# Raw x in the K, V and Q projections, the 1/rms row spread by TensorE, and one work unit per attention pair through all groups

## Chip, cores and metric

The kernel runs on all 8 cores of one Trainium2 chip (two dies, cores 0 to 3 and 4 to 7). The metric is the device time in microseconds (us) of the slowest core; "span" is a core's time from its first to its last instruction in the profiled run. A ratio is the mean time of one kernel's fast runs over the mean of the other's fast runs of the same rounds on the same chip, so it is not quite the ratio of the medians that are quoted.

## The reference, cut to what matters

Batch 4, 4096 tokens, width 1024. Two cores share a batch element: each takes every second tile of 128 queries (2048 tokens, four groups of 512), and both compute K and V for all 4096 tokens (eight blocks of 512).

```python
xn = rmsnorm(x, norm_mix_g)
u  = xn @ w_in                                # conv B,C,V | q | k | v | two gates
y_a = short_gated_conv(b_g, c_g, v_a, conv_w) @ w_a_out
o   = diff_attention(q, k, v, lam, slopes)    # 4 heads, 2 softmax maps of 64, ALiBi, causal
o   = rmsnorm(o, subln_g) * (1 - lam_init)
y_b = o @ w_b_out
x = x + (g_a * y_a + g_b * y_b) @ w_o         # g_a, g_b: sigmoid gates
h = rmsnorm(x, norm_mlp_g) @ w_mlp_in
x = x + jnp.square(jax.nn.relu(h)) @ w_mlp_out
return rmsnorm(x, norm_final_g)
```

## The kernel before

One list W holds the work other than attention as (weight, function) entries: K, V, Q and conv projections, then gates and merge. An attention group is a generator that gives control back twice per pair (one 128-key tile of both key halves against 512 queries of one head), and the loop then runs entries of W. All of them share PSUM bank 7 while a group runs; banks 0 to 3 hold scores, 4 to 6 the P·V sums. Cast loads (fp32 to bf16) go out on GpSimd's queue (`cload`), plain transfers on SyncE's (`ld`, S.dma("sp")).

```python
def row_bcast(blk, src, dst, n, p):             # the 1/rms row of a block, over HBM
    row = rr_sp[blk, 0:n]
    ...                                         # (cut)
            return e.dma_start(out=row.rearrange("(t p) -> p t", p=128), in_=src.ap[:, 0:4])
    S.dma("sp", w, [src], [key])
    ld(dst.ap, rr_sp[blk:blk + 1, 0:n].partition_broadcast(128), [dst], [key])

def prelude(blk):
    ...                                         # a: load x^T and tokens; sq: squares; r: 1/rms; b: row_bcast
    def nrm(c):                                 # x^T := x^T * gain * row, before any K, V or Q matmul
        ...
    steps = [a, sq(0), sq(1), sq(2), sq(3), r, b, nrm(0), nrm(2), nrm(4), nrm(6)]

def epilogue(h):                                # reads PSUM banks 4, 5, 6 throughout
    ...                                         # reciprocals of the row sums
    dve(... e_u = b5 * (-lam/l2) ...)
    for t in range(4):
        dve(... e_o[t] = oview(0, t) / l1 + e_u[t] ...)
    ...                                         # squares, 1/rms of the head output on GpSimd
    deferred.append((2, d1))                    # e_b = e_o * 1/rms
    deferred.append((4, d2))                    # four PE transposes, copy, store to on_sp

def merged(g, upto, ratio):
    oring[0] = Ring([7])
    credit = 0.0
    for slot in attn(g):
        run_deferred()
        credit += ratio / 2.0
        while credit >= 1.0:
            credit -= 1.0
            if done[0] < upto:
                one_chunk()
    oring[0] = ALL
PLAN = {0: ("a0", "a1", 1.4), 1: ("a1", "a2", 1.25), 2: ("a2", "a3", 0.8), 3: ("a3", "g2", 1.6)}
# after attention: all of W1 (8 MB as it lands) and W2[0] are loaded in one heap, then the rest of the gates,
# then W2[1..3], then x2 of block 0 (m_load(0)), then the MLP
```

The softmax here doesn't subtract the row's maximum and nothing guards it: scores larger than these inputs give would overflow.

## Time and profile before

| kernel before | us |
|---|---|
| median of the first runs (lowest, highest) | 1758.13 (1747.26, 1761.42) |
| first softmax exponential at | 147 |
| attention groups 0, 1, 2, 3 | 208, 197, 197, 341 |
| gates and merge left over | 207 |
| MLP | 451 |

The stage times are the stretches that the prediction shows. The page of the profile adds three lines that the prediction does not show: busy time and share of each engine, what the chain that ended last consisted of, and TensorE's granted clock in 40 equal slices of the span (tenths of full speed).

```profile
PE 1243.2 (71%) x7168; PEld 585.5 (33%) x7168; DVE 500.4 (29%) x1135; ACT 529.8 (30%) x744; POOL 61.6 (4%) x97
PE 58%; DMA 22%; DVE 10%; issue 4%; ACT 3%; POOL 1%; DVEq 0%; SPq 0%; ACTq 0%; POOLq 0%
PEclk9576567677777889776798998979769999999999
```

PE is the only engine over a third busy, and 22% of the chain is transfers. The clock reaches 9 for good only in the last quarter, the MLP.

### The profile page before, as it was taken

Reading aid. Unit: us, or ns where it says so; the run is one execution under the profiler, and the core shown is the slowest. Engines: PE = TensorE matmul, PEld = TensorE weight load, DVE = VectorE, ACT = ScalarE, POOL = GpSimd, SP = SyncE. Lnnn points to the kernel's source line nnn. Section 1 sums busy time; section 2 is a strip of 40 time slices with the busy share of each in tenths; the row PEclk is TensorE's granted clock in tenths of the full one; section 3 lists DMA queues with packets and bytes.
Section 4 is the critical chain, followed back from the end, with each engine's and each line's share of the span. In section 5 each row is a group of like instructions: output and inputs, shape, how many; then the busy total and the mean of one; then the engine's idle time right before and its main releaser. Section 6 shows DMA issues by size and latency. Waiting matters only on the chain.

```text
span 1748.7 us, 20490 instructions; the slowest of 8 cores (1730.7 to 1748.7 us)
## 1 busy us (share of the span) xinstructions
PE 1243.2 (71%) x7168; PEld 585.5 (33%) x7168; DVE 500.4 (29%) x1135; ACT 529.8 (30%) x744; POOL 61.6 (4%) x97
## 2 busy tenths in 40 slices
PE   3053255575746768785896986939439999999998
PEld 1021122232323334432343443414114444444443
DVE  1022245133433423321324234423302121221212
ACT  1011221153325635553464553212103022130220
POOL 2000000000000000000000001000000000000000
PEclk9576567677777889776798998979769999999999
DMA  8877210810312110724003014980760020120101
GB/s 169 84 83 76 69 40 19 97 56 11 85 26 55 37 11 28 111 47 102 27 35 114 1 52 133 183 209 33 161 164 13 37 85 1 48 73 37 61 1 61
DMA packets 38021, 119.57 MB, mean 68 GB/s; under 512 B 7680, under 2 KB 12160, under 8 KB 34464
## 3 DMA queue, kind: packets, MB, share of 16 engines
q0 software_dynamic: 7200, 39.91, 17.5%
q1 hardware_dynamic: 30720, 78.33, 14.0%
q8 instruction: 60, 0.98, 0.2%
q14 instruction: 41, 0.34, 0.1%
HBM read 128.77 MB, written 29.37 MB: 90 GB/s over the span
## 4 chain that ended last, share of the span: by engine, by line
PE 58%; DMA 22%; DVE 10%; issue 4%; ACT 3%; POOL 1%; DVEq 0%; SPq 0%; ACTq 0%; POOLq 0%
PE ps_all L386 57%; DMA rr_sp<-big 6%; DMA big<-rr_sp 5%; DMA big<-xs 5%; ACT big L670 2%; DMA big<-x_sp 2%; DMA x_sp<-big 1%; DMA xm_sp<-big 1%; DVE big L706 1%; DVE big L489 1%; DMA big<-xn_sp 1%; DVE big L830 1%; DVE big L710 1%; DMA big<-ya_sp 1%; DVE big L814 1%
## 5 line engine op out<-in xcount | busy, mean ns | idle before, releaser
L386 PE MATMUL ps_all<-big 128*128 128x512 bf16 (+4 forms) x6976 | 1229.5, 344 | 424.5 <-DVE big L564 66.4
L386 PEld LDWEIGHTS ps_all<-big 128*128 128x128 bf16 (+1 forms) x6976 | 573.8, 102 | 1074.5 <-issue 674.5
L670 ACT ACTIVATE big<-ps_all,big 128x1024 bf16<-128x1024 f32 (+3 forms) x384 | 320.2, 880 | 356.9 <-PE ps_all L386 340.0
L898 ACT ACTIVATE big<-ps_all 128x512 bf16<-128x512 f32 x128 | 76.4, 597 | 193.0 <-PE ps_all L386 193.0
L899 DVE TENSOR_TENSOR big<-big 128x512 bf16<-128x512 bf16 x128 | 54.4, 425 | 193.5 <-ACT big L898 193.1
L791 DVE SCALAR_TENSOR_TENSOR big<-big,ps_all 128x512 f32<-128x512 f32 x64 | 44.0, 688 | 190.0 <-PE ps_all L386 189.9
L780 ACT ACTIVATE big<-ps_all,big 128x512 f32<-128x512 f32 x64 | 44.0, 687 | 154.7 <-PE ps_all L386 154.7
L489 DVE SCALAR_TENSOR_TENSOR big<-big 128x512 bf16<-128x512 bf16 x56 | 39.2, 745 | 171.4 <-DMA big<-rr_sp 171.4
L915 ACT ACTIVATE big<-big 128x1024 bf16<-128x1024 f32 x16 | 16.9, 1057 | 208.3 <-DVE big L910 208.3
L430 ACT ACTIVATE big<-big 128x1024 bf16<-128x1024 f32 x32 | 33.8, 1057 | 129.1 <-DMA big<-xs 129.1
L910 DVE SCALAR_TENSOR_TENSOR big<-ps_all,big 128x512 f32<-128x512 f32 x32 | 24.0, 751 | 163.2 <-PE ps_all L386 163.2
L715 POOL TENSOR_TENSOR big<-big 128x4 f32<-128x4 f32 x16 | 16.2, 1015 | 784.5 <-DVE big L713 600.7
L818 ACT ACTIVATE big<-big 128x1024 bf16<-128x1024 f32 x16 | 16.9, 1057 | 81.2 <-DVE big L814 81.2
L675 DVE TENSOR_TENSOR big<-big 128x256 bf16<-128x256 bf16 x64 | 18.6, 290 | 73.6 <-ACT big L670 73.5
L814 DVE SCALAR_TENSOR_TENSOR big<-ps_all,big 128x512 f32<-128x512 f32 x32 | 22.1, 689 | 59.1 <-PE ps_all L386 35.0
L605 DVE TENSOR_TENSOR big<-ps_all,big 128x512 f32<-128x512 f32 x16 | 11.1, 692 | 87.5 <-PE ps_all L386 74.0
L828 PE MATMUL ps_all<-big 128*128 128x128 bf16 x128 | 10.5, 229 | 35.0 <-DVE big L817 30.4
L537 DVE CAST big<-ps_all 128x512 bf16<-128x512 f32 x32 | 21.8, 690 | 46.4 <-PE ps_all L386 46.4
L727 PE MATMUL ps_all<-big 128*128 128x128 bf16 x64 | 7.1, 242 | 38.0 <-DVE big L720 36.7
L554 DVE CAST big<-ps_all 128x512 bf16<-128x512 f32 x28 | 19.4, 691 | 29.7 <-PE ps_all L386 29.5
L830 DVE TENSOR_TENSOR big<-ps_all,big 128x1024 bf16<-128x1024 bf16 x16 | 19.6, 1224 | 23.4 <-DMA x_sp<-big 18.0
L917 POOL TENSOR_TENSOR big<-big 128x1 f32<-128x1 f32 x16 | 8.7, 543 | 459.5 <-DVE big L916 459.5
(69 smaller groups left out, 328.7 us busy)
## 6 DMA issues: line engine op xcount, KB each, us to landing
big<-xs SPq DMA_DIRECT2D x48, 512.0 KB, 4.5
xm_sp<-big SPq DMA_DIRECT2D x16, 512.0 KB, 2.9
big<-w POOLq DMA_DIRECT2D x8, 1024.0 KB, 34.3
big<-w POOLq DMA_DIRECT2D x4, 2048.0 KB, 24.2
big<-xm_sp SPq DMA_DIRECT2D x16, 512.0 KB, 4.7
out<-big SPq DMA_DIRECT2D x16, 512.0 KB, 2.6
big<-xT POOLq DMA_DIRECT2D x14, 512.0 KB, 15.6
xn_sp<-big SPq DMA_DIRECT2D x4, 1024.0 KB, 4.1
```

Source lines behind the costliest of these rows:

```text
L386: S.op("pe", lambda e: e.matmul(out, lhsT, rhs, start=start, stop=stop, skip_group_check=skip), reads, writes)
L430: act(lambda e: e.activation(junk.ap, xt.ap, AF.Square, accum_out=ss1[blk].ap[:, t:t + 1]), [xt], [junk, ss1[blk]])
L489: dve(lambda e, k=k: e.scalar_tensor_tensor(x[k].ap, x[k].ap, ccol(C_GMIX + k), R_b.ap, ALU.mult, ALU.mult), [x[k], cst, R_b], [x[k]])
L537: dve(lambda e: e.tensor_copy(dst.ap, ps), [key], [dst])
L670: act(lambda e, a=a, b=b, c=c, s=s, PT=PT, scale=scale: e.activation(PT.ap[:, :, a:b], Sb[s][:, :, a:b], AF.Exp, bias=ccol(C_BTAB + c), sc ...
L780: act(lambda e: e.activation(t.ap, ps, AF.Tanh, bias=hbg.ap[:, 8 * w + dm:8 * w + dm + 1], scale=0.5), [key, hbg], [t])
L791: dve(lambda e: e.scalar_tensor_tensor(t.ap, t.ap, 1.0, ps, ALU.add, ALU.mult), [key, t], [t])
L814: dve(lambda e: e.scalar_tensor_tensor(x.ap[:, hs], ps, 0.5, x.ap[:, hs], ALU.mult, ALU.add), [key, x], [x])
L830: dve(lambda e: e.tensor_tensor(g_x2.ap, pb, ccol(C_GMLP, 8).unsqueeze(2).to_broadcast([128, 8, 128]), ALU.mult), [key, cst], [g_x2])
L898: act(lambda e: e.activation(r.ap, ps, AF.Relu), [key], [r])
L899: dve(lambda e: e.tensor_tensor(h2[fc].ap, r.ap, r.ap, ALU.mult), [r], [h2[fc]])
L910: dve(lambda e: e.scalar_tensor_tensor(x.ap[:, hs], ps, r2q[b].ap[:, t:t + 1], x.ap[:, hs], ALU.mult, ALU.add), [key, x, r2q[b]], [x])
```

## The change

Its intent is to take the waits out of everything before the MLP. (1) K, V and Q use raw x; the gain is folded into the weights, and 1/rms is applied as results leave PSUM (V; Q; K of blocks 1 to 3) or as the exponential's scale (K of blocks 0, 4 to 7). (2) The row of 1/rms is spread over partitions by four small matmuls. Squares run one block ahead. (3) One unit of other work per pair, from the first pair to the last. (4) The epilogue copies the sums out of PSUM at once and does its arithmetic later. (5) SBUF is laid out per head, so W1 can come in as heads of group 3 end; all first loads are queued at once.

```diff
-N_DMA_SEMS = 12
+N_DMA_SEMS = 24
 ...
+    def bcast(blk):
+        def f():
+            ps, key = obank()
+            for t in range(4):
+                mm(ps[:, t * 128:(t + 1) * 128], rs1[blk].ap[:, t:t + 1].to_broadcast([128, 128]),
+                   ccol(C_ID, 128), t == 0, t == 3, [rs1[blk], cst], [key], skip=True)
+            dve(lambda e: e.tensor_copy(R_b.ap, ps), [key], [R_b])
 ...
+    def fold_gain(w, c):
+        dve(lambda e: e.tensor_scalar_mul(w[c].ap, w[c].ap, ccol(C_GMIX + c)), [w[c], cst], [w[c]])
+    def k_evac(blk, h, ps, key):
+        dst = KT[blk][h]
+        if blk in ksc:
+            dve(lambda e: e.tensor_copy(dst.ap, ps), [key], [dst])
+        else:
+            dve(lambda e: e.tensor_tensor(dst.ap, ps, R_b.ap, ALU.mult), [key, R_b], [dst])
 ... (V times rs1 and Q times R_b as they leave PSUM; block 4's K straight behind the loads)
+        for m in range(2):                                    # epilogue: three copies, L686 and L688
+            dve(lambda e, m=m: e.tensor_copy(o[:, m, 0:3, 0:129], bank(4 + m)... ), [pk(4 + m)], [o_raw])
+        dve(lambda e: e.tensor_copy(o[:, :, 3, 0:129], bank(6)... ), [pk(6)], [o_raw])
 ... (d0: combine the two maps; d1: squares and 1/rms; d2: product, L714; d3: transposes L722, copy, store)
+        deferred.extend([(1, d0), (2, d1), (4, d2), (5, d3)])
 ...
+    W += spread(qs(0), stats(5, 1))
+    mark(0)
+    W += spread(ks(5) + vs(5), [wc_load(0), wc_load(1)] + normed(0) + [lambda: xT_load(2, 2)])
+    W += spread([], stats(1, None))
+    W += [(0.2, bcast(1))]
+    W += spread(ks(1) + vs(1) + qs(1), [halo_load, wc_load(2), wc_load(3), halo_stat] + ...)
+    mark(1)
+    W += [(0.2, halo_norm)] + [(0.4, halo_chunk(ch)) for ch in range(4)]
+    W += spread(conv(0), normed(1) + stats(2, 6))
+    W += [(0, lambda: xT_load(6, 1)), (0.2, bcast(2))]
 ... (blocks 2, 6, 3, 7 in the same way)
+    W += [(0, g_w1)] + [(1, f) for f in conv(3)]
+    W += [(0, lambda: g_loads(0))]
+    W += [(1, f) for f in conv(2)] + [(0, g_w2)]
+    mark("G")
+    W += [(0, lambda: g_loads2(0))]                           # reload of attention and conv outputs, on_sp, ya_sp
+    W += G_list(0, 1) + G_list(1, 2) + G_list(2, 3)
+    mark("G3")
+    W += G_list(3, None)
 ...
+    for n, p in enumerate(pairs):
+        if n + 1 < len(pairs):
+            if pairs[n + 1]["g"] != p["g"]:
+                until(pairs[n + 1]["g"])                      # flush what the next group needs
+            qk(n + 1)
+            ex(n + 1)
+        pv(n, 0)
+        other(limit, 0.5)
+        pv(n, 1)
+        if p["last"]:
+            epilogue(g, p["h"])
+            if g == 3:
+                deferred.append((2, lambda h=p["h"]: w1_load(h)))
+        other(limit, 0.5)
+    oring[0] = Ring(list(range(8)))
+    run_deferred(True)
+    w2_load(0, 6)
+    m_load(0)
+    until("end")
```

## The prediction

> **What bounds the kernel now.** I read the busy time by stretches first, cut where the stages change (first and last softmax exponential, line L670, and the first matmul of the MLP). Columns: stretch, its length, busy us with instruction count of PE, PEld, DVE, ACT, POOL, then granted TensorE clock, DMA share, GB/s.
>
> ```profile
> 0.00:147.00 147.00, 43.22 (x162) 16.58 (x162) 23.61 (x49) 15.17 (x26) 15.45 (x30) 0.72 0.82 114
> 147.00:355.00 208.00, 97.46 (x560) 44.25 (x560) 70.87 (x198) 41.33 (x66) 9.93 (x13) 0.70 0.38 59
> 355.00:552.00 197.00, 125.37 (x818) 60.38 (x818) 74.92 (x197) 75.12 (x101) 8.23 (x10) 0.74 0.15 36
> 552.00:749.00 197.00, 144.06 (x1138) 76.81 (x1136) 65.64 (x181) 105.45 (x133) 7.73 (x10) 0.83 0.29 54
> 749.00:1090.00 341.00, 267.64 (x1872) 132.23 (x1871) 105.66 (x236) 167.07 (x212) 8.05 (x12) 0.85 0.21 63
> 1090.00:1297.00 207.00, 121.67 (x576) 54.62 (x575) 59.53 (x85) 31.18 (x48) 3.49 (x7) 0.80 0.69 149
> 1297.00:1748.00 451.00, 443.78 (x2048) 200.65 (x2048) 100.12 (x192) 94.46 (x160) 8.69 (x16) 0.99 0.13 45
> ```
>
> The stretches are: preamble; attention groups 0, 1, 2, 3 each with the projection work mixed into it (and flushed after it); the gate/merge work left over; the MLP. Only the MLP is at its limit: PE busy 444 of 451 us at clock 0.99. Before it, no engine is full in any stretch and the clock lies at 0.70 to 0.85. So these 1297 us are bound by waits. Which, the chain of waits in order of time (start, us, what) and the table of waits (total, times, longest) say:
>
> ```profile
> 56.52 13.82 DMA rr_sp<-big
> 70.41 15.02 DMA big<-rr_sp
> 109.23 13.98 DMA rr_sp<-big
> 123.28 20.69 DMA big<-rr_sp
> 322.88 20.66 DMA rr_sp<-big
> 343.61 8.46 DMA big<-rr_sp
> 1296.98 443.81 PE ps_all L386 x2048
> ...
> DVE big L489 <- DMA big<-rr_sp: 171.4, 7, 34.9
> PE ps_all L386 <- DVE big L564: 66.4, 8, 32.7
> PE ps_all L386 <- DVE big L706: 60.4, 12, 21.4
> PE ps_all L386 <- DMA big<-x_sp: 49.1, 1, 49.1
> PE ps_all L727 <- DVE big L720: 36.7, 4, 9.9
> ```
>
> First, each block's 1/rms row goes to HBM and comes back spread over 128 partitions, about 29 to 35 us each time, and x is normalised (L489) before any K, V or Q matmul can start. Second, L564 (Q's copy) is late for that reason. Third, the epilogue's reads of PSUM (L706, L720) hold PE at head and group ends. Fourth, the MLP starts 49 us late behind the reload of x2. What PE does when fed, a stretch of group 3 shows, same columns, and the unit costs of ACT:
>
> ```profile
> 1018.00:1055.00 37.00, 34.57 (x266) 17.11 (x265) 9.46 (x14) 22.47 (x24) 0.00 (x0) 1.00 0.22 76
> ...
> L670 ACT ACTIVATE big<-ps_all,big 128x1024 bf16<-128x1024 f32 x168 | 180.5, 1131 | 130.1 <-PE ps_all L386 129.8
> L670 ACT ACTIVATE big<-ps_all,big 128x512 bf16<-128x512 f32 x152 | 102.3, 703 | 158.9 <-PE ps_all L386 142.3 <-DVE big L730 10.6
> ```
>
> **What the Trainium skill says.** "TensorE: Matmul & The Clock Gate", part 1, says that PE runs at half clock after some 3.4 us of idleness and at full clock after as long busy. The trace agrees: 1.00 in the fed stretch, 0.70 where group 0 waits. A wait thus costs twice. The same part warns of 13/16 of the clock once three cores of a die run dense matmuls; here all eight run the MLP at 0.99, so the trace differs and I do not apply it. "Trainium Kernel Development and Optimization", Key Constraints, says that all queues' transfers run on the same 16 DMA engines and interleave; the trace fits, a 2 KB row write taking 14 us beside loads where 128 KB of normalised attention output takes 2.3. "DMA: Bandwidth & Descriptors", specifications, puts pieces under 512 B below line rate; the row write is one float per token.
>
> **Unit costs.** A 512-column matmul: 443.81/2048 = 0.217 us. A 129-column P·V matmul: 0.058 (four weight loads in 0.23 us in the fed stretch's timeline). Scores: two 64-row halves overlap, so 0.108 per 512 columns, 0.43 per full pair. A PE transpose: 0.61/8 = 0.076. The fed stretch holds 86, 132, 36 and 11 of these: 18.7 + 7.7 + 3.9 + 0.8 = 31.1 us in 37, so a merged loop reaches **0.84** of this ideal.
>
> **The change, part by part.** *Start.* K, V, Q are taken from raw x: the gain is folded into the weights (24 DVE multiplies of 0.35 us, 8 us, beside loads); V gets 1/rms as it leaves PSUM, Q and the K of blocks 1 to 3 get the row R_b, and the K of blocks 0 and 4 to 7 gets it as the exponential's scale. R_b comes from four small fp32 matmuls into one bank and one 0.69 us copy, an estimated 2 to 3 us instead of about 30. Eight row writes and seven wide reads go; so do the 24 normalisations of blocks 5 to 7 (24 × 0.745 = 18 us of DVE, off the path). All first loads are queued at once. Stated in program order, block 5's four squares come ahead of the first exponential, so six cast tiles (Wk, x4, Wv, x0, Wq, x5; 6.3 MB) and three blocks of tokens (6.3 MB) have to land. The cast queue spends 17.5% of 1749 us on 39.9 MB, 7.7 us per MB; the plain queue 14.0% on 78.3 MB, 3.1 us per MB. 48 + 20 + 8 us until the first lands = 76; the row and Q then make the first exponential **82**, against 147.2 now: −65.
>
> *Loop.* One work unit per pair through all 160 pairs, squares prefetched one block ahead. I counted which unit falls beside which pair: 160, 264, 384 and 500 projection matmuls beside groups 0 to 3 (P·V 160, 416, 672, 928; score columns in 512s 40, 104, 168, 232). Ideal: 35+9+4 = 48; 57+24+11 = 92; 83+39+18 = 140; 109+54+25 = 188. At 0.84: 57, 110, 167, 224. Group 0 is too short for its loads: x1, x2, four conv weights (5.2 MB cast, 40 us) and two to three token blocks (5 MB, 16 us), plus five units flushed through the single bank left to them at about 1.2 us extra: I put **80**. Group 1 with two flushed units 113, group 2 167, group 3 224. The epilogue now frees its PSUM banks after three copies (about 0.56+0.56+0.4 = 1.5 us) instead of reciprocals, products and four 0.35 us combinations (3.1 us plus queueing), so I allow only 10 us over the sixteen heads. Sum 594: the loop ends at 676; groups 0 to 3 take 943 us now.
>
> *Rest of the gates.* 580 matmuls stay behind: 126 us, twelve sets of eight transposes 7, waits for DVE between them 10 (1.5 to 4.4 us each at the ends of z in the trace), and 9 for the last 2 MB of W1, six W2 tiles and x2 on the DMA engines: **152**, to 828. Now the stretch is 207, of which 20 and 49 us are DMA trouble: W1 starts in one heap after attention, and x2's reload queues behind W2. The new SBUF plan is by head, so W1 comes in during group 3, and x2 of block 0 is loaded before the rest of the gates.
>
> *MLP.* Unchanged, 451 and 3 for entry: **454**, to 1282. The time of the profiled run lay 1.5 us above its span; rounded, **1285**. Gains: start 65, groups 128 + 84 + 30 + 107, rest 55.
>
> **Rivals.** (1) *DMA takes over.* Share times length summed before the MLP is 121+79+30+57+72+143 = 502 us of full engines, almost all of which stays; over 828 us that is 61%, so it does not bind on average, but early it does (0.82 in the preamble). If groups 0 and 1 each wait 30 us more: 1345. (2) *The loop keeps its old quality.* From 850 to 1080 us the same sum gives 158 of 230 us, 0.69, with head ends and waits included. At 0.69 for all groups, 468/0.69 = 678 instead of 594: 1370. For it: one bank for all loop work, which must be emptied before the next unit, and flushes at group changes. Against: a unit and the next are separated by P·V and scores (about 1.4 us), longer than the 0.69 us evacuation. (3) *ACT becomes the bound.* A full pair costs 2 × 1.13 us, in head 0 4 × 0.70, plus at most 0.69 for the unit: 2.95 to 3.5, against PE's 0.43 + 0.93 + 1.73 = 3.1, at 0.84 3.7. Only head 0 is near; +10. (4) *W2 comes late.* 26 of 32 tiles (6.8 MB, 52 us of casting) are loaded when the gates end, and the first output matmuls need them 32 × 8 × 0.217 = 55 us later: a stall of 0 to 15 us. (5) *A lower clock under density*: 13/16 would add over 150 us; the MLP's 0.99 speaks against it.
>
> **Range and chances.** Rivals 1, 2 and 4 all lengthen; shorter by up to 60 us is possible if group 0 isn't held by DMA and the loop reaches 0.9. So 1225 to 1370 around 1285. Even with the loop wholly unimproved, start and rest alone take off 7%, so faster is nearly sure.
>
> **What would show it.** Right: no row transfers; first exponential near 82 us; group 0 under 90 us; clock above 0.9 from group 1 on; PE waiting for L706's successors under 20 us in all; the wait before the MLP below 5 us. Wrong: ACT waiting for token loads in group 0, PE waiting for the copy of the single bank in most pairs (loop over 680 us), or a PE gap some 55 us into the MLP.

## The result, and the profile after

The changed kernel takes **1470.31 us** (median of 4 runs, 1469.95 to 1470.92), the kernel before in the same rounds 1756.52; ratio 0.838 (95%: 0.834 to 0.841). It is faster, as predicted, but 185 us above the predicted 1285 and outside the range of 1225 to 1370. On another chip the unaltered kernel gave 1465.81 (ratio 0.835). The outputs are right.

The busy time by stretches of the slowest core, columns as in the prediction: preamble, groups 0 to 3, gates left over, MLP.

```profile
0.00:74.00 74.00, 45.33 (x172) 18.70 (x172) 21.81 (x56) 15.28 (x26) 12.78 (x26) 0.83 0.97 205
74.00:172.00 98.00, 72.70 (x404) 33.74 (x400) 47.33 (x130) 33.26 (x46) 10.32 (x13) 0.74 0.41 91
172.00:321.00 149.00, 120.38 (x890) 62.89 (x890) 74.43 (x185) 78.86 (x104) 7.62 (x9) 0.84 0.17 50
321.00:516.00 195.00, 166.14 (x1278) 87.31 (x1274) 87.28 (x203) 121.53 (x152) 10.24 (x14) 0.95 0.31 68
516.00:822.00 306.00, 226.57 (x1738) 116.49 (x1738) 95.27 (x218) 166.87 (x202) 10.43 (x15) 0.90 0.31 70
822.00:1019.00 197.00, 141.75 (x681) 64.53 (x682) 73.97 (x103) 35.79 (x56) 2.46 (x5) 0.85 0.49 134
1019.00:1469.00 450.00, 442.07 (x2049) 200.20 (x2046) 101.63 (x195) 94.48 (x160) 9.39 (x17) 0.99 0.18 56
```

| stage, us | before | predicted | after | after − predicted |
|---|---|---|---|---|
| to the first exponential | 147 | 82 | 74 | −8 |
| group 0 | 208 | 80 | 98 | +18 |
| group 1 | 197 | 113 | 149 | +36 |
| group 2 | 197 | 167 | 195 | +28 |
| group 3 (with 10 for head ends) | 341 | 234 | 306 | +72 |
| gates left over | 207 | 152 | 197 | +45 |
| MLP | 451 | 454 | 450 | −4 |
| span | 1748 | 1282 | 1469 | +187 |

The start and the MLP came out as predicted. The groups shrank by 195 us instead of 349, and the gates by 10 instead of 55. Group 3 ends here, as in the prediction's stretches, where the last head's transposes run, some 11 us behind the last exponential (822 against 811 us; before, 1090 against 1078). The slowest core, 7, is one of two that ran part of groups 0 and 1 at a clock of 0.81 (see below): they took 98 and 149 us there, 94 to 96 and 144 to 148 on the six other cores, so about 6 us of the two groups' 54 are that. Engines, chain and clock of the page after:

```profile
PE 1214.9 (83%) x7202; PEld 583.9 (40%) x7202; DVE 501.7 (34%) x1087; ACT 546.1 (37%) x744; POOL 63.2 (4%) x97
PE 68%; DMA 11%; DVE 10%; issue 5%; ACT 4%; POOL 1%; DVEq 0%; SPq 0%; ACTq 0%; POOLq 0%
PEclk8877777999999996999899859998999999999999
```

The transfers' share of the chain halved, but it is not gone. In the clock line two dips stand out after the start: the 6 (slice 16, from 551 us) and the 85 (slices 23 and 24, from 808 us). The chain in order of time (start, us, what) and PE's table of waits (total, times, longest) name them:

```profile
557.48 27.79 DMA big<-ya_sp
...
823.98 13.14 DMA on_sp<-big
...
837.39 10.30 DMA big<-x_sp
...
1019.05 442.04 PE ps_all L396 x2048
```

```profile
PE ps_all L806 <- DVE big L795: 54.2, 7, 32.4
PE ps_all L396 <- DMA big<-ya_sp: 28.9, 1, 28.9
PE ps_all L722 <- DVE big L714: 26.4, 12, 7.9
PE ps_all L396 <- DVE big L686: 16.0, 14, 4.8
...
PE ps_all L396 <- DVE big L688: 13.1, 14, 1.0
...
PE ps_all L396 <- POOL big L436: 9.9, 2, 5.1
```

The row transfers of before are gone from both views. In their place stand: a single wait of 28.9 us in group 3 for a reload of the conv output (ya_sp, 0.5 MB); a wait of 32.4 us behind attention (L806 transposes the merged z; L795, named as its releaser, only hands on a wait for DMA); twelve waits of PE's transposes L722 for the product L714 just ahead of them; the copies at the head ends (L686, L688), 29 us over 14 heads; and two waits of 5 us for the block's 1/rms (L436), on which the row now hangs.

What surrounds the first two, the timeline shows (start, us, engine, line, what; in brackets how long the engine waited and for whom):

```profile
552.16 1.27 POOL L400 DMA_DIRECT2D big<-wg  x2 [20.06 <-PE ps_all L396]
553.42 0.54 POOL L400 DMA_DIRECT2D big<-wo  x1
...
557.48 0.32 SPq L403 DMA_DIRECT2D big<-ya_sp  x1
...
821.75 1.13 POOL L400 DMA_DIRECT2D big<-w  x2
...
837.39 18.28 SPq L403 DMA_DIRECT2D big<-x_sp  x4
```

Both times 3.5 to 4 MB of cast loads (counted as they land) go out a few microseconds ahead of a small plain transfer on which PE soon depends: gate and output weights at 552 ahead of the reload at 557; the last W1 tiles and six W2 tiles at 822 ahead of a store at 824, the x2 reload at 837 and the x tiles of the merge. From 560 to 580 us the DMA engines are all busy, PE runs nothing and its clock falls to 0.50. The reload took 27.8 us; the median of the 48 x tile loads of the same 0.5 MB is 6.1 us to landing. The trace's packet records say how the two queues shared the engines: from 560 to 580 us 275 packets of the cast queue moved 2.77 MB and 274 of the plain queue 0.66 MB, so the small transfers got every second packet and a fifth of the bytes.

### The profile page after: what moved, and what is told of

It is laid out like the page before. It is cut to its first block, busy times and chain, and to the rows that moved or that the text cites. A ratio compares the mean times of both kernels' runs of the same rounds, so it can differ in the third digit from the quotient of the medians.

```text
span 1469.4 us, 20538 instructions; the slowest of 8 cores (1444.3 to 1469.4 us)
## 1 busy us (share of the span) xinstructions
PE 1214.9 (83%) x7202; PEld 583.9 (40%) x7202; DVE 501.7 (34%) x1087; ACT 546.1 (37%) x744; POOL 63.2 (4%) x97
## 3 DMA queue, kind: packets, MB, share of 16 engines
q0 software_dynamic: 7200, 39.91, 16.4%
q1 hardware_dynamic: 25824, 76.53, 15.1%
## 4 chain that ended last, share of the span: by engine, by line
PE 68%; DMA 11%; DVE 10%; issue 5%; ACT 4%; POOL 1%; DVEq 0%; SPq 0%; ACTq 0%; POOLq 0%
PE ps_all L396 67%; ACT big L662 3%; DMA x_sp<-big 3%; DMA big<-xs 3%; DMA big<-ya_sp 2%; DMA big<-x_sp 1%; DVE big L769 1%; DVE big L686 1%; DMA on_sp<-big 1%; DMA big<-wk 1%; DVE big L705 1%; PE ps_all L806 1%; DVE big L725 1%; DVE big L714 1%; POOL big L710 0%
## 5 line engine op out<-in xcount | busy, mean ns | idle before, releaser
L396 PE MATMUL ps_all<-big 128*128 128x512 bf16 (+3 forms) x7010 | 1201.0, 338 | 164.6 <-DMA big<-ya_sp 28.9
L662 ACT ACTIVATE big<-ps_all,big 128x1024 bf16<-128x1024 f32 (+3 forms) x384 | 337.9, 926 | 181.2 <-PE ps_all L396 173.5
L769 DVE SCALAR_TENSOR_TENSOR big<-big,ps_all 128x512 f32<-128x512 f32 x64 | 44.0, 687 | 156.7 <-PE ps_all L396 156.5
L806 PE MATMUL ps_all<-big 128*128 128x128 bf16 x128 | 10.9, 235 | 55.0 <-DVE big L795 54.2
L710 POOL TENSOR_TENSOR big<-big 128x4 f32<-128x4 f32 x16 | 16.4, 1022 | 512.5 <-DVE big L708 441.3
L548 DVE TENSOR_SCALAR big<-ps_all,big 128x512 bf16<-128x512 f32 x32 | 23.7, 750 | 35.1 <-PE ps_all L396 35.1
L806 PEld LDWEIGHTS ps_all<-big 128*128 128x128 bf16 x128 | 8.4, 105 | 61.4 <-issue 61.4
L722 PE MATMUL ps_all<-big 128*128 128x128 bf16 x64 | 6.5, 228 | 26.5 <-DVE big L714 26.4
L669 DVE TENSOR_SCALAR big<-big 128x256 bf16<-128x256 bf16 x64 | 18.2, 285 | 26.0 <-ACT big L662 25.9
L808 DVE TENSOR_TENSOR big<-ps_all,big 128x1024 bf16<-128x1024 bf16 x16 | 19.6, 1225 | 17.8 <-DMA x_sp<-big 10.4
```

The source lines that it names most:

```text
L396: S.op("pe", lambda e: e.matmul(out, lhsT, rhs, start=start, stop=stop, skip_group_check=skip), reads, writes)
L548: dve(lambda e: e.tensor_scalar_mul(v_all[:, :, n, 0:128], ps.rearrange("p (h v) -> p h v", h=4), rs1[blk].ap[:, t:t + 1]), [key, rs1[blk] ...
L662: act(lambda e, a=a, b=b, c=c, s=s, PT=PT, scale=scale: e.activation(PT.ap[:, :, a:b], Sb[s][:, :, a:b], AF.Exp, bias=ccol(C_BTAB + c), sc ...
L769: dve(lambda e: e.scalar_tensor_tensor(t.ap, t.ap, 1.0, ps, ALU.add, ALU.mult), [key, t], [t])
L806: S.op("pe", lambda e, c=c: e.transpose(pb[:, c, :], g_xb.ap[:, c * 128:(c + 1) * 128], ident), [g_xb, cbf], [key])
L808: dve(lambda e: e.tensor_tensor(g_x2.ap, pb, ccol(C_GMLP, 8).unsqueeze(2).to_broadcast([128, 8, 128]), ALU.mult), [key, cst], [g_x2])
```

## The experiments

My first theory was that the miss is made of a few such waits: reload behind casts, loads behind casts at the end of attention, and transposes placed too close behind their product. The rival was that the loop itself is poor (PE held up by the single bank or by the order inside a pair), so that removing those waits moves the loss elsewhere. Four chips were used: A for the result, B for e1 to e4, C for e5 to e8, D for e9 to e16. e16 is the changed kernel unaltered, 1465.81 us on chip D; stages of one kernel repeated within a few us from chip to chip. The kernel before did not repeat as well (1744 us on C, 1767 on B), so across chips I compare times and not ratios. Time at half clock, where it is given, is summed from the clock records of the trace. Medians are those of the fast runs.

### The reload of the conv output

**e1_gl2_first**: the reload one entry ahead of the casts.

```diff
-    W += [(1, f) for f in conv(2)] + [(0, g_w2)]
-    W += [(0, lambda: g_loads2(0))]
+    W += [(1, f) for f in conv(2)] + [(0, lambda: g_loads2(0)), (0, g_w2)]
```

> Edit: the reload of the attention output and the conv output for the first gate group is put ahead of the 4 MB of gate and output weights on cast queue, which the changed kernel starts 3 us before it. In the changed kernel PE waits 28.9 us for that reload in group 3. Theory A (the reload is slow because it shares the 16 DMA engines with the cast loads started just before): the wait falls below 6 us and the kernel is 22 to 28 us faster (1442 to 1448). Theory B (the wait only moves, since the weights are now later and PE waits for them): less than 8 us faster.

Measured: 1465.78 us, ratio 0.830; the wait stayed at 30.2 us. The swap changed nothing: the casts still went out first, at 546 us, when PE's last conv matmul released their tiles, and the reload at 551: on SyncE's queue it stands behind the last store of group 2's conv output, and that store waits for the conv's last arithmetic. The order in the program set nothing between the two queues. As this kernel is in effect the unaltered one, it also serves as chip B's comparison.

**e5_gl2_early**: the reload stated two conv units earlier, so that it stands ahead of group 2's last store (what it reads, group 0's conv output, was stored long before).

```diff
+    c2 = [(1, f) for f in conv(2)]
+    W += c2[:10] + [(0, lambda: g_loads2(0))] + c2[10:] + [(0, g_w2)]
```

> Edit: the reload of the first gate group's attention and conv output stands two work units (some 7 us) earlier in program order, not just ahead of the weights' cast loads. The earlier run e1 left the wait at 30 us: the reload still went out behind the last stores of the conv output, 4 us after PE's last conv matmul had released the casts. Theory A (the reload loses against cast loads that start before it lands): started 7 us ahead it lands before them, the wait falls from 29 to below 6 us, group 3 is 22 to 28 us shorter. Theory B (the wait moves to the late gate weights): group 3 is less than 8 us shorter.

Measured: 1434.42 us, ratio 0.822. The timeline of e5 shows the order that e1 had wanted:

```profile
538.02 0.32 SPq L403 DMA_DIRECT2D big<-ya_sp  x1
...
543.85 1.28 POOL L400 DMA_DIRECT2D big<-wg  x2 [20.05 <-DMA big<-ya_sp]
```

The wait is gone and group 3 (measured to its last exponential from here on; the unaltered kernel has a median of 292 over the cores, 285 to 296) takes 261 to 265 us: about 30 us, as much as the wait. So the wait was a real loss, not a place where another loss showed. The reload, issued 6 us before the casts instead of 5 after, landed after 6.1 us instead of 27.8 and cost PE nothing.

### The wait behind attention

**e2_x2_split**: x2's destination as four buffers, so that its four loads need not follow one another.

```diff
-    m_x2 = [area(SET1, SET0).take("m_x2a", [4, 8, 128], BF16), ...]
+    ...  m_x2t.append([am2.take("%s%d" % (n, t), [8, 128], BF16) for t in range(4)])
```

> Edit: the MLP's x2 tile is booked as four buffers instead of one, so its four loads no longer wait for each other's landing; they stand where they stood, at the end of attention. In the changed kernel PE then waits 32 us. Theory S (the four loads, each waiting for the last, block the one DMA queue for 18 us and with it the loads of x behind them): the wait falls to some 14 us, 15 to 20 us faster. Theory C (the cast loads of W1 and W2 fill the DMA engines, whoever queues): no more than 5 us faster.

**e3_x2_late**: x2's load moved behind the last group's gates.

```diff
-    m_load(0)                       # right after attention
+    g3 = G_list(3, None)
+    W += g3[:26] + [(0, lambda: m_load(0))] + g3[26:]
```

> Edit: the reload of x2 for the MLP's first block is moved from the end of attention to behind the gates of the last group. Nothing else, the same W1 and W2 loads run at the end of attention. Theory S (the queue is blocked by the reload, which first waits 13 us for the store of the last attention output and then 18 us for itself): the 32 us wait at the end of attention falls below 8 us, 24 to 32 us faster. Theory C (cast loads fill the engines): the wait stays above 20 us.

Measured: e2 1460.37 and e3 1456.57 us, 5 and 9 us under e1 on the same chip; the wait fell from 32 to 25.0 and to 22.6 us. So x2's place in SyncE's queue is the smaller part; more than 20 us stay with x2 out of the way.

**e6_casts_late**: the last W1 tiles and W2's first six stated behind the first gates, twelve more W2 tiles held until the last merged x is stored.

```diff
-            if g == 3:
+            if g == 3 and p["h"] < 3:
...
+    until("G3")
+    w1_load(3)
     w2_load(0, 6)
     m_load(0)
     until("end")
-    w2_load(6, 12)
+    w2_load(6, 12, ["xmsp15"])      # "xmsp15": key of the last store of merged x
```

> Edit: the last 2 MB of W1, the first six W2 tiles and the reload of x2 are moved from the end of attention to the start of the last gate group, whose gates need no load for 45 us; and the next twelve W2 tiles, which start when the gates end, wait for the last store of x. Theory C (cast loads on the engines slow the loads of x behind which the output projection waits): the waits of 32 and 15 us after attention fall to below 5 us each, 35 to 42 us faster, unless W2 then comes late in the MLP (a wait of up to 10 us some 55 us into it). Theory M (they move with the casts): less than 15 us faster.

Measured: 1437.76 us, ratio 0.824; the stretch of gates (from the last exponential) fell from about 200 to 177 us (medians of the cores), the MLP unharmed (450). One wait of 15 us went, but the first stayed at 22.7 us, against what I had meant the edit to do: the casts still went out at 815 us. GpSimd had nothing else to do, so stating them later did not make them later. SyncE's table of waits shows whom they met this time, a store of merged x, behind which the next x tile stands on that queue:

```profile
SPq L143 <- DMA xm_sp<-big: 22.3, 1, 22.3
```

### The transposes at the head ends

**e4_epi_late**: product and transposes three half steps apart instead of one.

```diff
-        deferred.extend([(1, d0), (2, d1), (4, d2), (5, d3)])
+        deferred.extend([(1, d0), (2, d1), (4, d2), (7, d3)])
```

> Edit: the transposes that end a head's epilogue are put off by two half steps (one pair), so that they no longer come right behind the product that they read. In the changed kernel PE waits 26 us in 12 heads for that product. Theory H (the turn from head to head, with its waits and the half clock that follows them, is what makes the groups longer than predicted): those waits fall below 5 us, and the clock rises, 20 to 40 us faster. Theory N (the waits are short enough to be lost in other slack): less than 10 us.

Measured: 1438.60 us, ratio 0.814 (one further run is left out), 27 us under e1. PE's table of waits now has for the product only one, at the flush behind the last head, against 12 and 27.9 us in e1:

```profile
PE ps_all L722 <- DVE big L714: 7.9, 1, 7.9
```

Groups 0, 1, 2 became 6, 6 and 11 us shorter. The time at half clock in the four groups is 102 us, against 137 in the unaltered kernel (medians of the cores). In those waits PE ran nothing else, so a transpose that is due before its product holds up all matmuls stated behind it.

**e8_phase_b**: on e4, the unit as a whole behind both P·V halves.

```diff
-        other(limit, 0.5)           # after the first P·V half
+        other(limit, 0.0)
...
-        other(limit, 0.5)           # after the second
+        other(limit, 1.0)
```

> Edit, on top of e4: the work unit of a pair runs after both halves of P times V instead of between them, so at a head's end it stands between the last P times V and the first of the next head, where PE waits for the three copies out of PSUM (about 2 us a head). Theory H (the turn of heads): groups 1 and 2 get 2 us a head shorter, 10 to 25 us in all against e4. Theory N: groups 1 and 2 keep their 139 and 183 us within 2, or get longer as two units meet at the single bank in the gates.

Measured: 1468.08 us, ratio 0.841, slower than e4. Groups 1, 2, 3 are about 8, 6 and 12 us longer than in e4. The idea that a unit between the two halves hurts is refuted; of the two places tried, the old one is better.

### The three together

**e9_all**: e4, e5 and e6 together, with the casts held by a data dependency instead of by their place in the program.

```diff
+        cload(W1[k]..., [W1[k]], ["xmsp7"] if h == 3 else [])
...
+    until("G3")
+    w1_load(3)
+    w2_load(0, 6, ["xmsp7"])        # "xmsp7": store of merged x at the end of the second gate block
```

> Edit: e5 (the first gate group's reload two units earlier), e4 (a head's transposes one pair later) and e6 together, and the last 2 MB of W1 and the first six W2 tiles now wait for the last store of x of the second gate group: e6 had moved them in program order only, and the cast queue, which had nothing else to do, still issued them at the end of attention, with a wait of 23 us left. If the causes are separate, the gains add: 30 (e5) + 25 (e4) + 15 (done by e6) + 25 to 32 (the wait at the end of attention gone) = 95 to 102 us below the changed kernel, some 1370. If the DMA work only moves the waits elsewhere, above 1400.

Measured: 1360.21 us, ratio 0.774 (0.772 to 0.776; one slow run left out), 106 us under the control. The wait for z, 54.2 us in all before, is nearly gone:

```profile
PE ps_all L806 <- DVE big L795: 11.8, 7, 3.4
```

The gates left over fell to 157 us and group 3 to 259 (both cut at the last exponential). The gains add (30, 27 and some 45): the three waits were independent losses, and the rival is wrong as to them.

### What each part of the change is worth

**e7_row_hbm**: the row over HBM again, as before the change, for the four rows that are left.

```diff
-            ps, key = obank()
-            ... (four matmuls and the copy to R_b)
+            S.dma("sp", w, [rs1[blk]], [key])
+            ld(R_b.ap, rr_sp[blk:blk + 1, 0:512].partition_broadcast(128), [R_b], [key])
```

> Edit, an undo: the row of 1/rms goes to HBM and back as in the kernel before, at the place where the changed kernel has its four small matmuls; all else as changed. The changed kernel needs four such rows. Theory R (the row trip was a main part of the old time): each costs 15 to 30 us of stalled evacuation on the single bank, 50 to 110 us slower than the changed kernel. Theory P (the new order, with squares prefetched a block ahead, would hide it): under 25 us slower.

Measured: 1545.32 us, ratio 0.886 (one slow run left out). By stages: start +13, group 0 +14, group 1 +25, group 2 +24, 76 us in all; the whole is 80 us above the unaltered kernel on chip D. The row over TensorE is the largest part that I could separate.

**e10_w1_heap**: W1 in one heap after attention.

```diff
-            if g == 3:
-                deferred.append((2, lambda h=p["h"]: w1_load(h)))
...
+    for h in range(4):
+        w1_load(h)
```

> Edit, an undo of what the SBUF plan by head is for: all 8 MB of W1 load at the end of attention, as in the kernel before, and not after each head of group 3. Theory P (the plan is worth something): the wait for x behind the casts at the end of attention grows from 32 us to 60 or more, 20 to 45 us slower than the changed kernel, less the 8 us wait for the x2 store in group 3 that goes. Theory Q (the loads are hidden by the gates anyway): within 8 us of it.

Measured: 1488.91 us, 23 above the control (one slow run left out). The gates left over grew from about 200 to 234 us, and the wait behind attention from 32 to 63.6. Group 3 gained 7 us, in which PE's wait for L808, behind the store of x2, fell from 8.8 to 4.6; that W1's loads had slowed that store is likely, but not shown.

**e15_old_epi**: the epilogue of before, reading PSUM throughout, two deferred steps.

```diff
-        ... (three copies to o_raw; d0, d1, d2, d3)
+        ... (reciprocals, products and combinations from banks 4, 5, 6; d1, d2)
+        deferred.append((2, d1))
+        deferred.append((4, d2))
```

> Edit, an undo on the changed kernel: the head's epilogue as in the kernel before, reading the accumulators out of PSUM through reciprocals, products and combinations, with the old delays for its two last parts; all else as changed. Theory U (emptying PSUM first is a main part of the gain): 2 to 4 us a head and the clock, 40 to 80 us slower than the changed kernel. Theory V (the copies only replace one wait by another): within 15 us of it; the old delays even help the transposes as in e4.

**e16_control**: the changed kernel unaltered, on the same chip.

> The changed kernel itself, unaltered, beside the others on the same chip, as the base for their differences: 1465 to 1475 us, ratio 0.834 to 0.841 to the kernel before, groups 0 to 3 of 95, 145, 194 and 293 us and 203 us up to the MLP.

Measured: e15 1495.10 (two slow runs left out), e16 1465.81 us: 29 us, less than I expected. The table of waits of e15 has, for the last PSUM reader:

```profile
PE ps_all L397 <- DVE big L698: 63.0, 15, 8.2
```

against 31 us for the two copies in the control, so the copies save 32 us at the head ends; e15's transposes wait 12.7 instead of 27 us. In the four groups PE is idle 20 us longer in e15 and at half clock 34 us longer (medians of the cores). The new epilogue saved half of the wait for PSUM and at once doubled the wait of the transposes.

### How dense the loop can be

**e11_g3_denser**: on e9, 1.5 units per pair in group 3.

```diff
-        other(limit, 0.5)
+        other(limit, 0.5 if g < 3 else 0.75)
```

> Edit, on top of e9: one and a half work units per pair in group 3 instead of one, so that nearly all of the third gate group is done beside attention. Theory L (the loop is bound by what a pair has to wait for, so more work fits in): group 3 grows by less than the rest shrinks (about 32 units of 1.73 us = 55 us), total 10 to 25 us below e9. Theory T (PE is already the bound there, or units meet at the single bank): total within 8 us of e9, or above it.

Measured: 1412.41 us, with a **wrong result** (relative error 0.153): with group 3 denser, the reload, which lands in the tiles of group 2's output, goes out at 511 us, ahead of the store of group 2's last head at 519 (in e9 the store is at 507 and the reload at 514). That is a fault of my edit, and the likely cause of the error; the work is the same, so I use the times for the structure alone. Group 3 grew by about 90 us and the gates shrank by 38: 52 us worse than e9. More work per pair cost more inside the loop than outside; whether by its one bank or by PE's order is not shown.

**e12_dup**: four extra matmuls ahead of each unit of groups 0 and 1, result unchanged.

```diff
+        if start and not skip:
+            for _ in range(dup[0]):      # 4 while the units of groups 0 and 1 run
+                S.op("pe", ... same matmul, start=True, stop=True ...)
```

> Edit, on top of the changed kernel: each of the 52 work units of groups 0 and 1 starts with four more matmuls, thrown away, into its own bank (52 x 4 x 0.217 = 45 us more work for PE at full clock); results stay right. Theory K (the two groups are held by waits and by the half clock that follows from them, not by PE's work): groups 0 and 1 grow by less than 20 us together and their half-clock time (61 us of 242) falls by a third or more. Theory E (PE's own work is the bound, at whatever clock): they grow by 45 us or more.

Measured: 1500.83 us. The two groups hold 45 us more of ideal PE work and became 33 us longer; time at half clock in them fell from about 61 to 46 us (medians of the cores). About three quarters of added PE work shows: the groups are mostly a chain through PE, with some slack, and neither of the two pure readings is right.

### The row's place, and a version that beats both

**e13_bcast_early**: on e9, the squares of blocks 1, 2, 3 two to five units further ahead of the row that uses them.

```diff
-    W += spread(ks(5) + vs(5), [wc_load(0), wc_load(1)] + normed(0) + [lambda: xT_load(2, 2)])
-    W += spread([], stats(1, None))
+    W += spread(ks(5) + vs(5), [wc_load(0), wc_load(1)] + normed(0) + stats(1, None))
+    W += [(0, lambda: xT_load(2, 2))]
...
-    W += spread(conv(0), normed(1) + stats(2, 6))
+    W += spread(conv(0), stats(2, 6) + normed(1))
...
-    W += spread(conv(1), stats(3, 7))
+    c1 = conv(1)
+    W += spread(c1[:8], stats(3, 7)) + [(1, f) for f in c1[8:]]
```

> Edit, on top of e9: the four squares behind each row of 1/rms are put two to five work units ahead of the row's matmuls instead of right before them. In e9 one pair in each of groups 1 and 2 takes 12 to 13 us, and PE waits 5 us there for the power on GpSimd. Theory B (that wait, with its half clock, is lost time of the groups): groups 0, 1 and 2 get 4 to 9 us shorter each, 12 to 25 us in all (some 1340). Theory D (the time is the exponentials' or the loads', and returns elsewhere): less than 6 us.

Measured: **1350.01 us** (1349.65 to 1350.53), ratio 0.769 (0.767 to 0.771), 10 us under e9, a little less than expected; the waits for L436 are gone from PE's long ones, while that for the row's copy (L481) rose from 4.1 to 9.5 us. The edit also states block 2's x^T load behind the squares, so the 10 us belong to both moves. It is the best version, 120 us under the changed kernel of the diff (8%). Its groups 0 to 3 and the gates, in the same columns as above (slowest core; group 3 is cut here near the last exponential, at 738 us, not at the last head's transposes, at 753.5):

```profile
75.00:165.00 90.00, 65.27 (x401) 31.57 (x407) 47.92 (x130) 33.35 (x48) 10.32 (x13) 0.87 0.50 104
165.00:300.00 135.00, 109.98 (x870) 59.69 (x883) 72.36 (x182) 78.60 (x104) 7.29 (x8) 0.91 0.21 55
300.00:480.00 180.00, 157.29 (x1255) 85.00 (x1276) 86.91 (x202) 120.51 (x150) 10.51 (x14) 0.99 0.34 74
480.00:738.00 258.00, 211.53 (x1687) 112.08 (x1713) 89.15 (x198) 164.89 (x198) 9.17 (x13) 0.97 0.37 82
738.00:899.00 161.00, 140.59 (x706) 65.06 (x720) 82.07 (x129) 37.97 (x60) 2.69 (x4) 0.97 0.49 146
```

Nearly all the clock that the changed kernel lost in group 3 and in the gates (0.90 and 0.85) is back (0.97). Much of that half clock had lain inside the DMA waits themselves (0.50 from 560 to 580 us), where it cost nothing more: e5 gained no more than its wait.

**e14_act_copy**: on e13, one of the three copies at a head end on ACT.

```diff
-            dve(... e.tensor_copy(o[:, m, 0:3, 0:129], bank(4 + m) ...), m = 0, 1
+        dve(... bank 4 ...)
+        act(lambda e: e.copy(o[:, 1, 0:3, 0:129], bank(5) ...), [pk(5)], [o_raw])
```

> Edit, on top of e13: of the three copies that empty the accumulators at a head's end, one is done by ScalarE beside the other two on VectorE, so 1.1 us instead of 1.6 in a row. In e9 PE waits 5 to 6 us a group for them. Theory H (each head's turn is held by the copies): 0.5 us a head, 5 to 12 us faster than e13. Theory X (ScalarE is itself busy with the next head's exponentials at that moment): same within 4 us, or slower.

Measured: 1351.89 us, ratio 0.770 (one slow run left out): the same within 2 us. PE's waits for the copies stay at 25 us (27 in e13); splitting them over two engines is not what helps.

## Why the prediction was wrong

The direction, the start and the MLP were right; the size was wrong by 185 us. PE's own work came out as counted (e9's four groups hold 49, 92, 140 and 187 us of it by the prediction's unit times, against 48, 92, 140 and 188); what failed are the terms for waits: the 0.84 of the loop, the 10 us for head ends and the 9 us of DMA in the gates, and no term held the reload in group 3. By the prediction's own steps:

**Start, "the first exponential 82".** 74 us. Right in kind. The cast queue's packets took less over the whole run (16.4% of 1469 us for 39.9 MB, 6.0 us per MB, against the 7.7 taken from before); whether that is the 8 us was not looked at.

**"R_b comes from four small fp32 matmuls into one bank and one 0.69 us copy, an estimated 2 to 3 us instead of about 30."** Right in kind: the four copies last 0.69 us each, and no row goes over HBM. e7 puts it at 76 to 80 us. What the step left out is that the row hangs directly behind the squares and 1/rms of its block where the program states them together; pulling them apart gave 10 us (e13, with one x^T load moved too).

**"The epilogue now frees its PSUM banks after three copies … so I allow only 10 us over the sixteen heads."** This term failed by about 45 us: the copies hold PE for 29 us over 14 heads, and the transposes behind the product for 26 us in 12 waits. The sign asked for was under 20 us of wait for the copies; it was 29. I counted what left the PSUM path and did not look at where the deferred steps land on PE's own queue. e4 shows the second part, 27 us of time for 18 us of wait less. The first stayed in every version (e14).

**"152" for the rest of the gates, with "9 for the last 2 MB of W1, six W2 tiles and x2 on the DMA engines".** This term failed by 45 us. I charged the loads for their share of DMA time, as if PE paid only for bytes. What PE paid for was small plain transfers that queued beside 3.5 MB of casts, of which there are several in a row (a store, x2, x tiles). e2 and e3 show that x2's place is the smaller part, e9 that holding the casts takes about 45 us off the stretch.

**Rival 1, "DMA takes over", was placed in groups 0 and 1.** It came in group 3 and behind attention. The prediction names no reload in group 3 at all; that reload beside the casts cost 30 us (e5). The stages' DMA shares (0.31 in group 3) could not show it: a mean over 306 us hides 28 us of full engines.

**"At 0.84: 57, 110, 167, 224" for the loop.** This failed too, and only in part by the waits named so far. In e13, with most of them removed, groups 0 to 3 take 90, 135, 180 and, to the last head's transposes as in the prediction, 273 us: 678 in all against 594. The fed stretch from which 0.84 came held no group change, no wait for an epilogue's PSUM reads; in e9 the ideal content (49, 92, 140 and 187 us by PE's unit times) is 0.54, 0.67, 0.76 and 0.72 of the groups. Rival 2, "the loop keeps its old quality" at 0.69, gave 678 in all; it describes the loop better than my main line, and of the sign of being wrong half came true in the changed kernel: the loop took 748 us, over 680, though PE waited for the single bank in well under half of the 160 pairs (L725 14 times, L769 19). In e13 PE is busy 550 us in the four groups and idle 129. At the fed stretch's ratio of busy to ideal time (34.57 to 31.1) the 468 would be 520, so by this estimate some 30 of the 84 us are slower PE work, which the 71 us at half clock can account for, and some 55 are idle time beyond the 74 that the 594 left for it. What the idle time waits for, e13's table says:

```profile
PE ps_all L396 <- ACT big L662: 19.4, 33, 1.7
PE ps_all L396 <- DVE big L725: 15.2, 14, 2.6
PE ps_all L396 <- DVE big L686: 13.7, 14, 3.8
...
PE ps_all L396 <- DVE big L688: 13.1, 14, 1.0
PE ps_all L396 <- DVE big L769: 12.8, 18, 1.7
...
PE ps_all L396 <- DVE big L808: 10.0, 3, 7.0
PE ps_all L722 <- DVE big L714: 9.7, 2, 7.9
PE ps_all L396 <- DVE big L481: 9.5, 3, 3.2
```

L686 and L688 are the copies at head ends, L714 the flush behind the last head, L662 the exponentials. L725, L769, L808 and L481 each empty the one bank of the loop: 47.5 us, and some small ones beside them. So the single bank, the rival of my first theory, is not out of the case: no run gave the loop a second bank. The place of the unit in the pair (e8), the engine of the copies (e14) and lack of PE work (e12) are each tested and are not the remedy. Of the 84 us above the prediction the copies make up 17 (27 less the 10 allowed) and the last flush 8; what makes up the remaining 60 or so stays **open**.

**ACT, W2 late, 13/16 clock.** As predicted, ACT did not bind (PE's waits for it: 15.3 us, none over 1.7), although its exponentials grew from 1131 to 1177 ns for a full tile, and no gap appears 55 us into the MLP. The 13/16 clock did show: the clock records of cores 6 and 7 hold 124 us at 0.8125 between 71 and 232 us in the profiled run, those of the other cores and of all sixteen experiments none. The prediction looked for it only in the MLP (0.99) and missed it in its own trace: in the profiled run of the kernel before, cores 0 to 3, 6 and 7 have it for 97 us or more from about 315 us on, core 2, which the stretches show, for 215 us up to 878 us. So not all of the low clock in those stretches was waiting; from 500 to 850 us it was 0.78 on cores 2 and 3 and 0.83 or 0.84 on the six others. In the changed kernel it cost little, some 6 us in groups 0 and 1, far from the 150 us of rival 5: core 6's span of 1455.7 us lies in the middle of the eight, core 7's is 6 us above that of core 3, which did not show it.

The sum: of 187 us, e5 accounts for 30, the casts behind attention for about 45, the transposes for about 25, the row's place for 10: some 110 shown, and e13 as a whole takes away 120. The 67 us that are left are those 84 in the four groups, less 17: start, gates and MLP of e13 (75, about 146 behind the last transposes, 450) come to 671 us against the 688 predicted.

**Where the gain of 286 us came from**: the row (76 to 80, e7), the epilogue (29, e15), W1 by head (23, e10). The other 150 us, among them the first loads queued at once, the squares one block ahead and one unit per pair in place of the old plan, were not separated, and the parts need not add.

## What to carry to other kernels

When big loads and small latency-critical transfers share the DMA engines, ask at each release of a big buffer which small transfer PE will need next, and hold the big loads by a data dependency; their place in the program did nothing here on a queue that was otherwise empty (e6). A deferred step that ends on PE must be due later than its producer's finish, since all that PE has behind it waits too. An efficiency taken from a fed stretch (0.84) was more than any whole group of the loop reached (0.54 to 0.76, e9); take it from a whole group, and look at the longest single waits, not at mean DMA shares.

## What the Trainium skill lacked or had wrong

- "DMA: Bandwidth & Descriptors", Queues, rings and completion order, says that an engine goes round-robin between rows of queues packet by packet; the counts of packets from 560 to 580 us agree with it (275 of the cast queue, 274 of the plain one). It has no figure for what that does to a small plain transfer beside cast loads: here 0.5 MB took 27.8 us beside 4 MB of casts, against a median of 6.1 us for loads of that size over the run, and holding the casts was worth 45 us (e9).
- No page that I read has a cost for the cast itself: the cast queue's packets took 6.0 us of all 16 engines per MB landed (16.4% of 1469 us for 39.9 MB), the plain queue's 2.9 (15.1% for 76.5 MB).
- None of them says that stating a load later does not delay it on an idle queue: in e6 the moved casts went out at 815 us all the same; with a dependency (e9) the wait fell from 22.7 to 3.4 us.
- "TensorE: Matmul & The Clock Gate", part 1, puts a whole die at 13/16 of the clock once three cores run dense matmuls, for as long as the load lasts. Here the kernel before showed it on all four cores of one die and on two of the other (97 to 225 us each, in the attention groups), the changed kernel on cores 6 and 7 alone for 124 us in one profiled run, the control on none, and the MLP of all eight ran at 0.99. Its half clock after idleness agrees: the clock was 0.50 in the 20 us in which PE waited for the reload.
